# Gate blocks of one branch moved beside the mixers' small work, and moments before centring in the norms

## The chip, the cores and the metric

One core of a Trainium2 chip runs the whole kernel. The metric is the device time of one execution in microseconds (us). Three runs of the kernel before gave a median of 1899.39 us.

## The reference

Two layers of a hybrid decoder trunk work on 280 columns: 16 meta tokens, 256 prompt positions and 8 samples that each carry their own recurrent states. The stream has 1024 channels.

```python
proj = x @ w_in                       # 128 blocks of 128 columns, and dt
m_z, m_xbc, m_dt, h_q, h_f, h_i, h_g, r_q, r_k, r_v, r_g, gates = split(proj)
y_m = mamba_branch(m_z, m_xbc, m_dt, ...)      # conv, chunked recurrence, norm
y_h = hgrn_branch(h_q, h_f, h_i, h_g, ...)     # 8 heads, chunks of 32
y_r = retention_branch(r_q, r_k, r_v, r_g, ...)  # 4 heads, 256 x 512 states
g_m, g_h, g_r = split(sigmoid(gates))
mixed = g_m*(y_m @ w_br_m) + g_h*(y_h @ w_br_h) + g_r*(y_r @ w_br_r)
x = layer_norm(ALPHA*x + mixed @ w_out)
x = layer_norm(ALPHA*x + (silu(x @ w_g) * (x @ w_u)) @ w_ffn_out)
```

An input layer norm stands ahead of layer 0. All states go back to memory.

## The kernel before, in words

Channels lie on the 128 partitions and the 280 columns along the free axis; the second layer drops the 16 meta columns where it can, so that a product there has 264 columns. A weight block is 1024 x 128 values, 512 KB. `wblock` (line 204) loads it on SP's queue, ScalarE copies it to a rounded part `wh`, and VectorE subtracts to get the rest, `wl`. A block of products is 24 matmuls (wh by x, wl by x, wh by the rest of x), all from `large` (line 160). PSUM holds three such blocks (`pp`). The two layers run the same code.

**Stages of a layer.** First the convolution inputs (16 blocks, with 6 blocks of the first HGRN heads between them). Then four *pairs* p = 0 to 3 (line 1404): two HGRN heads and one Mamba-2 group are mixed, written as generators `hgrn` and `mamba`, while the projections of the next pair are computed: 6 HGRN blocks, 2 blocks of z and 2 of the HGRN gate; for p = 3 the first retention head's 8 blocks. Then retention: heads 1 to 3 are projected (8 blocks each), head by head is mixed (`ret_mix`), and `ret_samples` streams 8 states of 512 KB per head in and out of memory. In the slot of h = 3 stand the 8 blocks of the Mamba-2 branch's product (line 1445), whose results ScalarE copies out of PSUM. After them come 8 blocks of that branch's gates (`sigmoid_pair`), four multiplications on GpSimd that join the two (line 1451), the gates and product of the HGRN branch, the retention branch, the output projection, the norm, and the feed-forward layer.

**What sets the order.** `tick()` (line 260) is called in the middle and at the end of each block; each generator on the plan advances by its rate, steps over halves. `finish()` runs what is left without blocks between. The small matmuls of a step are pinned behind the large matmul issued last (`put`, line 162). The order within an engine is fixed when the program is built; an engine does not pass an instruction that waits.

**Smooth gates.** z and the HGRN gate are computed with exponentials and a logarithm (`smooth_pair`, line 819): two copies out of PSUM, then Abs, Exp, Ln on ScalarE, one two-input operation on VectorE, and Exp; z is also multiplied once more. The two blocks of z are the last but two of a pair, and the two of the HGRN gate are the last.

**Norms.** `inv_std` (line 445) squares the mean on ScalarE, takes the mean from the first two channel blocks, forms the variance, and takes the mean from the next two while ScalarE computes Ln and Exp. `scaled` (line 357) then scales block by block and splits into two parts; `opening` (line 228) starts the next stage's first three weight blocks on the channel blocks as they come. At the very end `norm` scales in place and stores.

Of the kernel before, what the change touches and what calls it, by code (L numbers as in the profile page):

```python
# [18 lines left out]
OPEN = 3  # L19
# [13 lines left out]
KB = 8  # L33
# [4 lines left out]
T = TP + NS  # L38
# [17 lines left out]
def _in_order():  # L56

    run = lambda off, n: [off + P * i for i in range(n)]
    o = []
    for p in range(4):  # L60
        heads = [c for off in (OFF_HF, OFF_HQ, OFF_HI) for c in run(off + 256 * p, 2)]
        if p == 0:
            for j, n in enumerate(MIX):
                o += run(OFF_XBC + 256 * j, 2) + heads[:n]
                del heads[:n]
        o += heads + run(OFF_Z + 256 * p, 2) + run(OFF_HG + 256 * p, 2)
    for h in range(4):
        o += run(OFF_RQ + 256 * h, 2) + run(OFF_RK + 256 * h, 2) + run(OFF_RV + 512 * h, 4)
    return o + run(OFF_GM, 8) + run(OFF_GH, 8) + run(OFF_GR, 8) + run(OFF_RG, 16)


IN_ORDER = _in_order()
# [16 lines left out]
def body(ctx: ExitStack, tc: tile.TileContext, a: dict):  # L89
# [48 lines left out]
    def copy(out, in_):  # L138
        return S.activation(out, in_, AF.Copy)  # L139
# [61 lines left out]
    fence, hold = [], []  # L201


    def wblock(src, nk):

        src_ = wraw.tile([P, RC, P], F32, tag="raw", name="raw")
        load(out=src_[:, :nk, :], in_=src)
        hi = whp.tile([P, RC, P], F32R, tag="wh", name="wh")
        lo = wlp.tile([P, RC, P], F32R, tag="wl", name="wl")
        with tc.high_priority(offset=boost):  # L210
            copy(hi[:, :nk, :], src_[:, :nk, :])
            ins = sub(lo[:, :nk, :], src_[:, :nk, :], f32(hi[:, :nk, :]))
        if fence:
            nosync(raw(ins), fence.pop())
        return hi, lo
# [7 lines left out]
            if k == nk // 2 - 1:  # L223
                tick()

    opened, norm_end = [], []

    def opening(srcs, c0):

        ps = [pp.tile([P, 512], F32, tag="pp", name="pp")[:, c0:T] for _ in srcs]  # L230
        ws = [wblock(src, KB) for src in srcs]
        for j in range(4):
            for p, w in zip(ps, ws):
                for k in (2 * j, 2 * j + 1):
                    for part in w:
                        large(p, part[:, k, :], blk(xhl[0], k)[:, c0:T], k == 0 and part is w[0], False)
        for j in range(3):
            for p, w in zip(ps, ws):
# [5 lines left out]
        opened.extend(ps)  # L244
        fence[:] = norm_end

    boost = BOOST[0]
# [109 lines left out]
    def scaled(x, rs, gk, bk, vec, less):  # L357

        nonlocal xhl
        new = tuple([pair("px", dt=F32R) for _ in range(4)] for _ in range(2))  # L360
        c = slice(lead, T)
        sca = chained()

        def full(b, e):
            xi = x[b // 2][:, b % 2, c]
            (vec if e is V else sca)(affine(xi, xi, gk, bk, b, e))

        def upper(b, e):
            xi = x[b // 2][:, b % 2, c]
            ins = (vec if e is V else sca)(affine(new[0][b // 2][:, b % 2, c], xi, gk, bk, b, e))  # L370
            if e is S:
                run["ops"].append(ins)

        def lower(j):
            return vec(sub(new[1][j][:, :, c], x[j][:, :, c], f32(new[0][j][:, :, c])))

        def times(j):
            vec(mul(x[j][:, :, c], x[j][:, :, c], b2(rs)))

        with tc.high_priority(offset=AHEAD):  # L380
            vec(mul(x[0][:, 0, c], x[0][:, 0, c], rs))
            upper(0, V)
            vec(mul(x[0][:, 1, c], x[0][:, 1, c], rs))
            upper(1, S)
            times(1)
            upper(2, S)
            upper(3, S)
            hold[:] = [run["ops"][-1]]
            full(0, V)
            less(2)  # L390
            times(2)
            full(1, S)
# [27 lines left out]
    def ln_input(x):  # L420

        first = flat("pm", P)
        G.memset(first, 1.0 / P)
        m1, mu, m2 = (mxt()[:, :T] for _ in range(3))
        mm(m1, first, x[0][:, 0, :], True, True)
        for j in range(4):
            sub(x[j], x[j], b2(m1))
            sq = pair("pm")
            S.activation(sq, x[j], AF.Square)
            if j % 2:  # L430
                total = pair("pm")
                add(total, x[j - 1], x[j])
                for i in range(2):
                    ins = mm(mu, onesd, total[:, i, :], j == 1 and i == 0, j == 3 and i == 1)
            if j < 3:
                add(sq[:, 0, :], sq[:, 0, :], sq[:, 1, :])
                mm(m2, onesd, sq[:, 0, :], j == 0, False)
            else:
                for i in range(2):
                    ins = mm(m2, onesd, sq[:, i, :], False, i == 1)  # L440
        keep_warm(14, ins)
        rs = tt_()
        scaled(x, rs, "lnin_g", "lnin_b", *inv_std(rs, mu, m2, x))

    def inv_std(rs, mu, m2, x):

        c = slice(T - rs.shape[1], T)
        vec = chained()

        def less(j):  # L450
            vec(sub(x[j][:, :, c], x[j][:, :, c], b2(mu)))

        with tc.high_priority(offset=AHEAD):
            S.activation(rs, mu, AF.Square)
            less(0)
            vec(sub(rs, m2, rs))
            vec(V.tensor_scalar(rs, rs, 0.0, None, ALU.max))
            rstd_of(rs, rs, 1.0, 0)
            less(1)
        return vec, less  # L460

    class Residual:
# [37 lines left out]
        def norm(self, gk, bk, out=None):  # L500
# [4 lines left out]
                return scaled(self.x, rs, gk, bk, vec, less)  # L505
            for j in range(4):
                x = self.x[j]
                if j > 1:
                    less(j)
                vec(mul(x[:, :, c], x[:, :, c], b2(rs)))  # L510
                for i in range(2):
                    ins = affine(x[:, i, c], x[:, i, c], gk, bk, 2 * j + i, S if i else V)
                    if i == 0:
                        vec(ins)
                store(out=out[j], in_=x[:, :, c])

    ln_input(x0)
# [292 lines left out]
    def sigmoid_pair(l, tag, silu=False):  # L810
# [5 lines left out]
                mul(t[:, i, lead:T], t[:, i, lead:T], ps)  # L816
        return t

    def smooth_pair(l, tag, silu):

        c = slice(lead, T)
        x, t = pair("pb"), pair(tag)
        for i in range(2):
            copy(x[:, i, c], in_block(l, lead))
# [555 lines left out]
    for l in range(L):  # L1380
# [20 lines left out]
        hp = hgrn_gate(l, 0, tiles)  # L1401
        z, hg = smooth_pair(l, "py", True), smooth_pair(l, "py", False)
        td = []
        for p in range(4):
# [12 lines left out]
        res = [[] for _ in range(4)]  # L1417

# [14 lines left out]

        rps = [rp]
        begin(retention(), 4 * NR, 64)
        for h in range(4):
            if h < 3:
                rps.append(ret_proj(l, h + 1, tab))
                if h == 0:
                    if l == 0:  # L1440
                        bounds()
                    begin(samples(), 4 * NSR, 122)
            else:
# [6 lines left out]
        for j in range(4):  # L1450
# [203 lines left out]
```

## Time and profile before

| | before |
|---|---|
| runs | 1896.95, 1899.39, 1900.35 us |
| the profiled execution | 1897.69 us |
| its span | 1895.6 us |
| TensorE busy (PE) | 1827.3 us |
| VectorE busy (DVE) | 1353.2 us |
| ScalarE busy (ACT) | 1090.3 us |
| GpSimd busy (POOL) | 374.6 us |
| mean granted TensorE clock | 0.989 of full speed |

The span runs from the first to the last instruction of the profiled execution; the other 2.1 us lie around it. The profiled execution is 1.7 us under the median of the runs. The granted clock has two levels in these rows: 1.00 is 2.4 GHz and 0.50 is 1.2 GHz. The order of the stages in time: the input norm to 20 us, convolution inputs to 104, pairs of layer 0 to 345, retention and merging to 725, output projection and feed-forward to 961, and the same again for layer 1.

### The profile page before, as it was taken

What the parts mean: (1) busy time and instruction counts of PE and PEld (TensorE: products, weight loads), DVE (VectorE), ACT (ScalarE), POOL (GpSimd) and SP (SyncE); (2) the same over time, 40 slices, a digit from 0 to 9 for tenths busy, and PEclk for the clock granted to TensorE, in tenths of its full rate; (3) what the DMA queues carried; (4) which work ended last, traced back from release to release, by engine and by line L of the source; (5) the groups of instructions that cost most, each with busy time, mean ns of one, the idle gap of its engine ahead of it and who ended that gap; (6) DMA issues with size and microseconds to landing.
All of it is one profiled execution on the core that took longest, in us unless ns stands there. A gap on an engine that the chain in (4) does not pass through costs nothing.

```text
span 1895.6 us, 38951 instructions
## 1 busy us (share of the span) xinstructions
PE 1827.3 (96%) x15744; PEld 1702.4 (90%) x15744; DVE 1353.2 (71%) x2183; ACT 1090.3 (58%) x1861; POOL 374.6 (20%) x415
## 2 busy tenths in 40 slices
PE   8989999999999999999999889999999999999997
PEld 7987788899888999999999778888988999999997
DVE  7898879766755766655478979996767567666654
ACT  6686677545555544544366857775455556454443
POOL 2032424211011023000220333342110100221001
PEclk9999999999999999999999989999999999999998
DMA  6545655556788744555545356555667886545563
GB/s 208 184 141 199 214 203 175 199 203 224 244 282 285 278 167 147 176 170 173 170 139 184 112 198 226 186 192 204 204 227 263 296 306 229 181 149 189 180 175 103
DMA packets 114995, 378.42 MB, mean 200 GB/s; under 512 B 13056, under 2 KB 18560, under 8 KB 114816
## 3 DMA queue, kind: packets, MB, share of 16 engines
q1 hardware_dynamic: 114816, 375.94, 59.1%
q8 instruction: 124, 2.03, 0.4%
q14 instruction: 55, 0.45, 0.1%
HBM read 317.61 MB, written 58.28 MB: 198 GB/s over the span
## 4 chain that ended last, share of the span: by engine, by line
PE 78%; DVE 11%; ACT 4%; DMA 3%; issue 2%; POOL 2%; DVEq 0%; ACTq 0%; POOLq 0%; SPq 0%
PE pp L160 63%; PE mx L169 9%; PE po L169 2%; PE vb L169 2%; DVE wl L142 2%; DVE pm L142 2%; DMA st<-s_ret 1%; DVE pa L142 1%; POOL hpt L142 1%; DMA ret_s<-st 1%; DVE py L154 1%; PE mx L172 1%; ACT wh L139 1%; DVE st L154 1%; DVE py L142 1%
## 5 line engine op out<-in xcount | busy, mean ns | idle before, releaser
L160 PE MATMUL pp<-px,wh 128*128 128x280 f32 (+1 forms) x5504 | 1119.0, 295 | 11.9 <-ACT pa L1090 5.7
L160 PEld LDWEIGHTS pp<-px,wh 128*128 128x128 f32 x5504 | 889.0, 190 | 29.8 <-issue 14.8
L142 DVE TENSOR_TENSOR wl<-raw,wh 128x1024 fp32r<-128x1024 f32 (+1 forms) x472 | 590.7, 1253 | 331.8 <-ACT wh L139 327.6
L160 PE MATMUL pp<-px,wl 128*128 128x280 f32 (+1 forms) x2752 | 796.7, 291 | 0.0
L139 ACT ACTIVATE wh<-raw 128x1024 fp32r<-128x1024 f32 (+1 forms) x472 | 493.8, 1048 | 349.8 <-PE pp L160 239.3
L160 PEld LDWEIGHTS pp<-px,wl 128*128 128x128 f32 x2752 | 521.9, 190 | 4.3 <-issue 0.8
L160 PE MATMUL pp<-py,wh 128*128 128x280 f32 (+1 forms) x1984 | 383.4, 289 | 0.8 <-ACT py L139 0.8
L160 PEld LDWEIGHTS pp<-py,wh 128*128 128x128 f32 x1984 | 313.7, 188 | 3.8 <-ACT py L139 1.3
L160 PE MATMUL pp<-py,wl 128*128 128x280 f32 (+1 forms) x992 | 285.2, 288 | 0.0
L160 PEld LDWEIGHTS pp<-py,wl 128*128 128x128 f32 x992 | 186.6, 188 | 0.7
L142 POOL TENSOR_TENSOR pa<-pa 128x280 f32<-128x280 f32 (+3 forms) x56 | 75.2, 1353 | 362.3 <-DVE pa L142 257.1
L169 PE MATMUL mx<-pm 128*32 128x16 f32 (+8 forms) x1728 | 116.6, 231 | 8.2 <-POOL pm L142 6.9
L769 ACT ACTIVATE st<-st 128x1024 f32<-128x1024 f32 x64 | 67.8, 1059 | 94.9 <-DMA st<-s_ret 62.7
L169 PEld LDWEIGHTS mx<-pm 128*32 128x32 f32 (+2 forms) x1728 | 87.5, 131 | 29.6 <-POOL pm L142 7.5
L154 DVE SCALAR_TENSOR_TENSOR st<-vb,qks,st 128x512 f32<-128x512 f32 x128 | 91.2, 745 | 23.7 <-PE vb L169 23.2
L142 DVE TENSOR_TENSOR pm<-pm 128x64 f32<-128x64 f32 (+7 forms) x179 | 85.9, 502 | 14.5 <-ACT pm L736 8.4
L142 DVE TENSOR_TENSOR pa<-pa,pp 128x280 f32<-128x280 f32 (+1 forms) x152 | 65.9, 433 | 37.0 <-PE pp L160 25.3
L142 POOL TENSOR_TENSOR pa<-px 128x560 f32<-128x560 f32 (+1 forms) x16 | 25.4, 1586 | 305.0 <-DVE py L142 304.8
L132 ACT ACTIVATE pm<-pm 128x544 f32<-128x544 f32 (+4 forms) x112 | 58.0, 540 | 13.2 <-DVE pm L154 13.1
L132 ACT ACTIVATE pa<-pp 128x280 f32<-128x280 f32 (+1 forms) x124 | 47.3, 385 | 28.8 <-PE pp L160 28.7
L139 ACT ACTIVATE pa<-pp 128x280 f32<-128x280 f32 (+1 forms) x80 | 31.4, 392 | 39.7 <-PE pp L160 39.6
L154 DVE SCALAR_TENSOR_TENSOR st<-vh,qks,st 128x128 f32<-128x128 f32 x128 | 39.7, 370 | 19.5 <-POOL st L142 11.7
(252 smaller groups left out, 1871.9 us busy)
## 6 DMA issues: line engine op xcount, KB each, us to landing
raw<-w_in SPq DMA_DIRECT2D x256, 512.0 KB
raw<-w_ffn_in SPq DMA_DIRECT2D x88, 512.0 KB
st<-s_ret SPq DMA_DIRECT2D x64, 512.0 KB
ret_s<-st SPq DMA_DIRECT2D x64, 512.0 KB
vh<-rows SPq DMA_DIRECT2D x64, 256.0 KB
raw<-w_br_r SPq DMA_DIRECT2D x32, 512.0 KB
raw<-w_ffn_out SPq DMA_DIRECT2D x32, 512.0 KB
st<-s_ssm SPq DMA_DIRECT2D x16, 512.0 KB
```

The costliest lines, as they stand in the source:

```text
L132: ins = S.activation(out, in_, func, **kw)
L139: return S.activation(out, in_, AF.Copy)
L142: return e.tensor_tensor(out, x, y, op)
L154: return V.scalar_tensor_tensor(out, x, s, y, op0, op1)
L160: place[0] = raw(TE.matmul(out, lhsT, rhs, start=start, stop=stop, skip_group_check=True))
L169: return put(TE.matmul(out, lhsT, rhs, start=start, stop=stop, skip_group_check=True))
L172: return put(TE.transpose(out, x, ident))
L769: S.activation(st, st, AF.Copy, scale=gam)
```

## The change

The input weights are stored in a new order, and so are the blocks. After the blocks of z and the HGRN gate of pairs 1 to 3 stand two blocks of the Mamba-2 branch's gates, and the last two stand after the first retention head. They are only copied out of PSUM (`plain_pair`); a new generator turns them into gates by the smooth way while retention head 1 is projected. The product of the Mamba-2 branch moves from the slot of h = 3 to h = 1, ahead of the projection of head 2, and is multiplied into the gates straight from PSUM. The rates follow: the pairs' generators run over 23 halves for 19, the retention's samples over 106 for 122. In the norms the variance is formed before any mean is taken off, and the second subtraction moves behind the first scaling. The input norm centres all four blocks in another order and issues the first three weight blocks itself, two behind the last square and one behind the last exponential. The last norm puts most of its scaling on ScalarE.

```diff
 (_in_order, pairs)
         o += heads + run(OFF_Z + 256 * p, 2) + run(OFF_HG + 256 * p, 2)
+        if p:
+            o += run(OFF_GM + 256 * (p - 1), 2)
     for h in range(4):
+        if h == 1:
+            o += run(OFF_GM + 768, 2)
...
 (wblock)
-            copy(hi[:, :nk, :], src_[:, :nk, :])
+            ins = copy(hi[:, :nk, :], src_[:, :nk, :])
+            if behind_ is not None:
+                nosync(raw(ins), raw(behind_))
 (opening)
-        ws = [wblock(src, KB) for src in srcs]
+        ws = ahead or [wblock(src, KB) for src in srcs]
 (scaled)
             upper(1, S)
+            less(1)
             times(1)
 (ln_input)
+        centre(0)
+        centre(1)
+        mean(0)
+        centre(2)
+        centre(3)
+        squares(0)
+        mean(1)
+        squares(1)
+        squares(2)
+        for i in range(2):
+            ins = mm(m2, onesd, sq[3][:, i, :], False, i == 1)
+        last_sq = squared[-1]
+        ahead.extend(wblock(a["w_in"][0, b], KB, last_sq) for b in range(OPEN - 1))
         keep_warm(14, ins)
         rs = tt_()
-        scaled(x, rs, "lnin_g", "lnin_b", *inv_std(rs, mu, m2, x))
+        how = inv_std(rs, mu, m2, x)
+        fence[:] = norm_end
+        ahead.append(wblock(a["w_in"][0, OPEN - 1], KB, run["ops"][-1]))
+        scaled(x, rs, "lnin_g", "lnin_b", *how)
 (inv_std)
             S.activation(rs, mu, AF.Square)
-            less(0)
             vec(sub(rs, m2, rs))
             vec(V.tensor_scalar(rs, rs, 0.0, None, ALU.max))
             rstd_of(rs, rs, 1.0, 0)
-            less(1)
+            norm_end[:] = [less(0)]
 (norm, the last)
-                if j > 1:
-                    less(j)
                 vec(mul(x[:, :, c], x[:, :, c], b2(rs)))
+                if j < 3:
+                    less(j + 1)
                 for i in range(2):
-                    ins = affine(x[:, i, c], x[:, i, c], gk, bk, 2 * j + i, S if i else V)
+                    ins = affine(x[:, i, c], x[:, i, c], gk, bk, 2 * j + i, V if i == 0 and j == 3 else S)
 (the layer)
-            begin(hgrn(l, p, hp, hg, oh), NH, 19)
-            begin(mamba(l, p, td, dd, xm, bc, z, ym), NM + 2 * (p == 0), 19)
+            begin(hgrn(l, p, hp, hg, oh), NH, 23)
+            begin(mamba(l, p, td, dd, xm, bc, z, ym), NM + 2 * (p == 0), 23)
             if p < 3:
                 hp = hgrn_proj(l, p + 1)
                 z, hg = smooth_pair(l, "py", True), smooth_pair(l, "py", False)
+                gm.append(plain_pair(l, pair("py")))
                 finish()
             else:
...
                 rp = ret_proj(l, 0, tab)
+                gm.append(plain_pair(l, pair("py")))
...
+        def gates_m():
+            for j in range(4):
+                for _ in range(2):
+                    yield 1
+                x, t = gm[j], pair("py")
+                smooth(x, t)
+                gm[j] = t
         for h in range(4):
+            if h == 0:
+                gms = begin(gates_m(), 8, 14)
+            if h == 1:
+                while len(ym) < 4 or gms in plan:
+                    tick()
+                block = branch(l, a["w_br_m"], ym)
+                for b in range(8):
+                    g = gm[b // 2][:, b % 2, lead:T]
+                    mul(g, g, block(b))
             if h < 3:
                 rps.append(ret_proj(l, h + 1, tab))
...
-                    begin(samples(), 4 * NSR, 122)
-            else:
-                mixed = pairs("pa", 4)
-                block = branch(l, a["w_br_m"], ym)
-                for b in range(8):
-                    copy(blk(mixed, b)[:, lead:T], block(b))
+                    begin(samples(), 4 * NSR, 106)
         boost = BOOST[2]
-        gm = gates(l)
-        for j in range(4):
-            mul(mixed[j][:, :, lead:T], mixed[j][:, :, lead:T], gm[j][:, :, lead:T], G)
+        mixed = gm
```

## Rows read from the trace of the kernel before

**Rows 1.** The page: busy time, share of the span and instructions of each engine.
```profile
PE 1827.3 (96%) x15744; PEld 1702.4 (90%) x15744; DVE 1353.2 (71%) x2183; ACT 1090.3 (58%) x1861; POOL 374.6 (20%) x415
```

**Rows 2.** Windows: stretch, its length, busy time by engine, granted clock, DMA share, GB/s.
```profile
core 0: us, PE busy (x) PEld busy (x) DVE busy (x) ACT busy (x) POOL busy (x), PEclk, DMA share, GB/s
100.00:345.00 245.00, 228.18 (x2521) 196.99 (x2520) 213.31 (x436) 169.57 (x379) 88.64 (x88) 0.98 0.57 191
1040.00:1305.00 265.00, 245.39 (x2643) 211.69 (x2642) 235.94 (x470) 186.17 (x409) 95.21 (x99) 0.96 0.57 192
655.00:725.00 70.00, 70.00 (x545) 69.76 (x544) 45.23 (x52) 34.71 (x43) 12.95 (x8) 1.00 0.51 172
```

**Rows 3.** Waits of PE over the span: who waited for whom, us in total, times, longest.
```profile
PE mx L169 <- DVE pm L142: 10.8, 7, 4.3
PE po L172 <- DVE pq L142: 7.3, 4, 2.7
PE mx L169 <- POOL pm L142: 6.9, 4, 4.2
PE pp L160 <- ACT pa L1090: 5.7, 2, 4.5
...
PE mx L172 <- ACT pm L139: 2.8, 2, 2.4
```

**Rows 4.** Windows of PE alone: the stretches of the mixers at half clock.
```profile
179.19:182.61 3.42, 3.42 (x16) 0.50 0.25 63
231.60:237.22 5.62, 5.62 (x18) 0.50 0.31 117
...
1094.90:1100.79 5.89, 5.66 (x31) 0.50 0.17 67
...
sum 28.59, PE 28.36; mean PE 4.05
```

**Rows 5.** Timeline at the end of pair 1: start, us, engine, line, operation, idle before.
```profile
223.30 1.90 POOL L142 TENSOR_TENSOR st<-st,dab 128x1024 f32<-128x1024 f32 x1
223.47 2.33 DVE L142 TENSOR_TENSOR py<-py 128x560 f32<-128x560 f32 x1
...
231.60 2.21 PE L169 MATMUL mx<-pm,ones 128*128 128x280 f32 x4 [4.27 <-DVE pm L142]
```

**Rows 6.** Timeline at the start of pair 1.
```profile
178.01 0.74 DVE L154 SCALAR_TENSOR_TENSOR py<-pb,py 128x560 f32<-128x560 f32 x1 [0.41 <-ACT py L132]
...
179.13 0.59 PE L172 MATMUL po<-ident,pa 128*32 128x128 f32 x2 [2.19 <-DVE pq L142]
```

**Rows 7.** Groups of instructions over the span: busy us, mean ns, idle before.
```profile
L142 DVE TENSOR_TENSOR wl<-raw,wh 128x1024 fp32r<-128x1024 f32 (+1 forms) x472 | 590.7, 1253 | 331.8 <-ACT wh L139 327.6
...
L142 DVE TENSOR_TENSOR pa<-pa,pp 128x280 f32<-128x280 f32 (+1 forms) x152 | 65.9, 433 | 37.0 <-PE pp L160 25.3 <-ACT pa L132 10.9
...
L132 ACT ACTIVATE py<-py,eps 128x560 f32<-128x560 f32 (+1 forms) x16 | 11.9, 745 | 0.1
```

**Rows 8.** The chain that ended last, in the feed-forward layer: start, us, what.
```profile
765.09 195.13 PE pp L160 x1512
```

**Rows 9.** Windows at the start and in the second layer's sample states; columns as in Rows 2.
```profile
5.00:10.00 5.00, 2.51 (x6) 1.78 (x6) 4.77 (x10) 2.29 (x4) 0.00 (x0) 1.00 1.01 341
...
1440.00:1593.00 153.00, 152.80 (x1266) 138.76 (x1266) 102.10 (x132) 88.34 (x126) 13.56 (x10) 1.00 0.85 293
```

**Rows 10.** Timeline of the input norm.
```profile
16.38 2.35 DVE L142 TENSOR_TENSOR wl<-raw,wh 128x1024 fp32r<-128x1024 f32 x2
...
19.71 0.37 PE L160 MATMUL pp<-px,wh 128*128 128x280 f32 x1 [2.30 <-DVE px L343]
```

**Rows 11.** Timeline of the norm between the layers.
```profile
962.17 0.74 DVE L142 TENSOR_TENSOR pa<-pa,mx 128x560 f32<-128x560 f32 x1 [0.99 <-ACT tt L454]
...
971.11 0.39 PE L160 MATMUL pp<-px,wh 128*128 128x280 f32 x1 [0.25 <-ACT px L342]
```

**Rows 12.** Timeline of the last norm, VectorE.
```profile
1883.78 0.70 DVE L142 TENSOR_TENSOR pa<-pa,mx 128x528 f32<-128x528 f32 x1 [0.93 <-ACT tt L454]
...
1891.62 0.42 DVE L343 TENSOR_SCALAR pa<-pa,par 128x264 f32<-128x264 f32 x1
```

More of the change, by code (lines that the diff above doesn't have):

```diff
@@ L66, in _in_order @@
         o += heads + run(OFF_Z + 256 * p, 2) + run(OFF_HG + 256 * p, 2)
+        if p:
+            o += run(OFF_GM + 256 * (p - 1), 2)
     for h in range(4):
+        if h == 1:
+            o += run(OFF_GM + 768, 2)
         o += run(OFF_RQ + 256 * h, 2) + run(OFF_RK + 256 * h, 2) + run(OFF_RV + 512 * h, 4)
-    return o + run(OFF_GM, 8) + run(OFF_GH, 8) + run(OFF_GR, 8) + run(OFF_RG, 16)
+    return o + run(OFF_GH, 8) + run(OFF_GR, 8) + run(OFF_RG, 16)
 IN_ORDER = _in_order()
@@ L201, in body, with wblock @@
     fence, hold = [], []
-    def wblock(src, nk):
+    def wblock(src, nk, behind_=None):
         src_ = wraw.tile([P, RC, P], F32, tag="raw", name="raw")
@@ L224, in project @@
                 tick()
-    opened, norm_end = [], []
+    opened, norm_end, ahead = [], [], []
     def opening(srcs, c0):
         ps = [pp.tile([P, 512], F32, tag="pp", name="pp")[:, c0:T] for _ in srcs]
-        ws = [wblock(src, KB) for src in srcs]
+        ws = ahead or [wblock(src, KB) for src in srcs]
         for j in range(4):
@@ L244, in opening @@
         opened.extend(ps)
+        ahead.clear()
         fence[:] = norm_end
@@ L425, in ln_input, with centre, mean, squares @@
         mm(m1, first, x[0][:, 0, :], True, True)
-        for j in range(4):
[L427 to L437, printed above, removed]
-            else:
-                for i in range(2):
-                    ins = mm(m2, onesd, sq[:, i, :], False, i == 1)
+        vec = chained()
+        sq, total = pairs("pm", 4), pairs("pm", 2)
+        squared = []
+        def centre(j):
+            vec(sub(x[j], x[j], b2(m1)))
+            squared.append(S.activation(sq[j], x[j], AF.Square))
+        def mean(j):
+            vec(add(total[j], x[2 * j], x[2 * j + 1]))
+            for i in range(2):
+                mm(mu, onesd, total[j][:, i, :], i + j == 0, i + j == 2)
+        def squares(j):
+            vec(add(sq[j][:, 0, :], sq[j][:, 0, :], sq[j][:, 1, :]))
+            mm(m2, onesd, sq[j][:, 0, :], j == 0, False)
+        centre(0)
[7 more added lines that the diff above has]
+        squares(2)
+        for i in range(2):
+            ins = mm(m2, onesd, sq[3][:, i, :], False, i == 1)
+        last_sq = squared[-1]
+        ahead.extend(wblock(a["w_in"][0, b], KB, last_sq) for b in range(OPEN - 1))
         keep_warm(14, ins)
         rs = tt_()
-        scaled(x, rs, "lnin_g", "lnin_b", *inv_std(rs, mu, m2, x))
+        how = inv_std(rs, mu, m2, x)
+        fence[:] = norm_end
+        ahead.append(wblock(a["w_in"][0, OPEN - 1], KB, run["ops"][-1]))
+        scaled(x, rs, "lnin_g", "lnin_b", *how)
     def inv_std(rs, mu, m2, x):
@@ L450, in less @@
         def less(j):
-            vec(sub(x[j][:, :, c], x[j][:, :, c], b2(mu)))
+            return vec(sub(x[j][:, :, c], x[j][:, :, c], b2(mu)))
         with tc.high_priority(offset=AHEAD):
             S.activation(rs, mu, AF.Square)
-            less(0)
             vec(sub(rs, m2, rs))
@@ L507, in norm @@
                 x = self.x[j]
-                if j > 1:
-                    less(j)
                 vec(mul(x[:, :, c], x[:, :, c], b2(rs)))
+                if j < 3:
+                    less(j + 1)
                 for i in range(2):
-                    ins = affine(x[:, i, c], x[:, i, c], gk, bk, 2 * j + i, S if i else V)
-                    if i == 0:
-                        vec(ins)
+                    ins = affine(x[:, i, c], x[:, i, c], gk, bk, 2 * j + i, V if i == 0 and j == 3 else S)
                 store(out=out[j], in_=x[:, :, c])
@@ L817, in sigmoid_pair, with plain_pair, smooth @@
         return t
+    def plain_pair(l, x):
+        for i in range(2):
+            copy(x[:, i, lead:T], in_block(l, lead))
+        return x
     def smooth_pair(l, tag, silu):
+        return smooth(plain_pair(l, pair("pb")), pair(tag), silu)
+    def smooth(x, t, silu=False):
         c = slice(lead, T)
-        x, t = pair("pb"), pair(tag)
-        for i in range(2):
-            copy(x[:, i, c], in_block(l, lead))
         S.activation(t[:, :, c], x[:, :, c], AF.Abs)
@@ L1403, in body @@
         td = []
+        gm = []
         for p in range(4):
-            begin(hgrn(l, p, hp, hg, oh), NH, 19)
-            begin(mamba(l, p, td, dd, xm, bc, z, ym), NM + 2 * (p == 0), 19)
+            begin(hgrn(l, p, hp, hg, oh), NH, 23)
+            begin(mamba(l, p, td, dd, xm, bc, z, ym), NM + 2 * (p == 0), 23)
             if p < 3:
@@ L1441, in body @@
                         bounds()
-                    begin(samples(), 4 * NSR, 122)
-            else:
-                mixed = pairs("pa", 4)
-                block = branch(l, a["w_br_m"], ym)
-                for b in range(8):
-                    copy(blk(mixed, b)[:, lead:T], block(b))
+                    begin(samples(), 4 * NSR, 106)
         boost = BOOST[2]
-        gm = gates(l)
-        for j in range(4):
-            mul(mixed[j][:, :, lead:T], mixed[j][:, :, lead:T], gm[j][:, :, lead:T], G)
+        mixed = gm
         yh = [split(o) for o in oh]
```

## The prediction

> **What bounds the kernel now.** I read the page's busy times first, then windows by stage, then PE's waits, then the timeline around the longest of them. TensorE is busy for 1827.3 of 1895.6 us [rows 1], and the change neither adds nor drops a matmul of a block: 24 matmuls follow each other at 195.13 / 1512 = 0.129 us, 3.1 us a block, wherever nothing small lies between [rows 8]. So a gain can only come from idle or slow TensorE. The windows show where that is: in the pairs of layer 0 PE is busy for 228.2 of 245 us and in those of layer 1 for 245.4 of 265, 16.8 + 19.6 = 36.4 us idle, while a stretch in the late gates has none [rows 2]. The mean clock of both pair stages is below 1.00 as well. Seven stretches, each right after a long wait, run at 0.50, that is 1.2 GHz, 28.6 us in all [rows 4]; at full clock the same work takes half of that, so they cost up to 14.3 us. The two together, 50.7 us, are what the pair stages have to give.
>
> The waits by partner [rows 3], with the 2.5 us of the input norm taken off the first row, and half of each slow stretch [rows 4] put to the wait that it follows, make four sorts:
> - *Before the pairs*: waits for ACT at L1090, 5.7 us, with one slow stretch of 3.4 us: 5.7 + 1.7 = 7.4 us.
> - *At the start of a pair*: a transpose into the shared PSUM tile waits for DVE's `pq`, 7.3 us in 4 waits, and another for ACT's `pm`, 2.8 us; four slow stretches of 3.4 us follow: 10.1 + 6.8 = 16.9 us.
> - *At the end of a pair*: the sums of squares of the norms wait for DVE, 10.8 - 2.5 = 8.3 us, with one slow stretch of 5.6 us: 8.3 + 2.8 = 11.1 us.
> - *In the middle*: matmuls wait for GpSimd's products, 6.9 us, with one of 5.9 us: 6.9 + 2.9 = 9.8 us.
>
> **The change part by part.** *Gate blocks in the pairs.* Each pair gets two blocks more, 6.2 us of TensorE, taken from the late gates, where PE never idles: the work itself nets to zero. Each block brings its load on SP's queue (512 KB at a DMA share of 0.57 [rows 2], 4.2 MB a layer), a ScalarE copy and a subtraction of 1.25 us on DVE [rows 7]. DVE is busy for 213 of 245 us there [rows 2]; a pair gets 2.5 us more of it beside 6.2 us of PE. The generators' steps now come every 23/17 = 1.35 halves for 1.12.
>
> By counting ticks from the code, a start-of-pair wait changes like this. Mamba's second step, whose DVE results are awaited, stays on tick 3; HGRN's third step, whose transpose waits, goes from tick 4 to tick 5: another half block, 1.56 us, lies between. The second reason is in the timeline: DVE reaches `pq` late since the smooth operation of the gate just projected stands in front of it and itself waits 0.41 us for ACT; PE then waits 2.19 us [rows 6]. With the two plain blocks last in a pair, that chain (Abs, Exp, Ln of 0.75 us [rows 7], the DVE operation of 0.74 us, Exp) is over two blocks earlier. Bounds: no gain, or all 16.9 us. I take three quarters, 12.7, as spacing alone covers 1.56 of each wait and a wait that falls away takes its slow stretch with it.
>
> End of a pair: the last steps keep their spacing in ticks (square to sum is two ticks before and after), but the smooth chains no longer fall among them. DVE's backlog there has another part, though: an operation that takes 2.33 us beside a GpSimd product on the states, against 0.74 us for a like one elsewhere [rows 5, 11]. That stays. Bounds 0 and 11.1; I take half, 5.5. Middle: the steps from GpSimd's products to their readers lie 4 ticks apart, as before; bounds 0 and 9.8, I take 2. Before the pairs nothing changes: 0. Against this stand new waits that a new order brings: nothing in the trace shows them; the bounds are nothing and the longest wait but one, 4.2 us [rows 3], in each layer. I take 3 for both. Net: -12.7 - 5.5 - 2 + 3 = -17.2 us.
>
> *Smoothing, product and joining.* The gates take four two-block chains a layer: four ScalarE operations of at most 0.75 us [rows 7] and one of 0.74 us on DVE [rows 6] each, spread over 16 halves of retention head 1. They replace eight sigmoids. The product's eight multiplications read PSUM at 0.43 us each on DVE [rows 7] for eight ScalarE copies, and GpSimd loses four. DVE and ACT have time in those stages; cost 0. Without this cover it would be 8 x 0.43 = 3.5 us a layer. The loop that waits for the Mamba results and the gates turns zero times: 20 + 16 = 36 ticks have passed and the slower generator needs 23. Of the 22 `py` slots I count at most 21 in use.
>
> *Retention order and samples.* Head 2 is projected 8 blocks later, so one slot of 16 halves has no retention steps, and head 3 is mixed beside the HGRN gates; these are blocks all the same, 0. The samples run 36 steps in 106 halves for 122: 2.94 halves a step. Per step that is 1.05 MB of states and 1.47 blocks of 0.52 MB, 1.82 MB. At 3.39 halves and 293 GB/s a step now takes (1.05 + 0.89) MB / 293 = 6.6 us, 1.3 more than its 3.39 x 1.56 us of blocks: that is the small matmuls. So in samples alone a step will take 2.94 x 1.56 + 1.3 = 5.9 us, at 309 GB/s against 293 at a share of 0.85 now, in a stretch with 0.2 us of PE idle; the start of the kernel moved 341 at a share of 1.01 [rows 9]. There is room, but less. Bounds 0 and 12 us (below); I take +1.5.
>
> *Input norm.* PE starts its first block at 19.71; two subtractions, 2.35 us, stand in DVE's way just before [rows 10]. By an estimate from those rows the first block could start some 3.1 us earlier: 1.6 us of the two subtractions lie behind the exponential, 0.66 us come from the variance's new place (as below), and some 0.8 from sums that end earlier and a ScalarE that is free for Ln. But the third weight's subtraction (1.2 us) and one centring (0.7 us) now fall into the chain that feeds the later channel blocks. 3.1 - 1.9 = 1.2; I take -1.3, as a short cast (0.1 us of it) leaves that chain (bounds -3.1 and +0.5).
>
> *Norms within.* The variance no longer waits for a centring of 0.74 us [rows 11], 0.66 us as its successor starts: the first matmul comes 0.66 earlier. But one centring of 0.73 us comes back between the first and the second scaling. PE's later wait, at 971.11 for the seventh channel block [rows 11], is fed by that chain: 0.07 us later. Three norms: +0.2 (bounds -2 and +2).
>
> *Last norm.* Its chain loses the same 0.66 us and three scalings on DVE (0.42 us long, about 0.35 each in the chain), and gains a centring of 0.70 [rows 12]: -0.66 - 1.05 + 0.70 = -1.0 (bounds -1.7 and 0).
>
> **Sum.** -17.2 + 1.5 - 1.3 + 0.2 - 1.0 = -17.8 us. The profiled execution took 1897.7, its span and 2.1 us around it: 1879.9. The median of the runs is 1.7 above the profiled execution: 1881.6, rounded to 1882.
>
> **The rivals.** *Blocked by GpSimd.* The 2.33 us at the end of pair 1 begin 0.17 us after GpSimd's product of 1.90 us and end 0.6 us after it [rows 5]. If such blocking, and not the smooth chains, makes DVE late, it stays, since the change moves none of the products on the states. Then only the spacing pays, at the start of pairs, on the four waits for `pq`: 1.56 off each of three and all of the shortest, 0.67, which makes 5.3 us, and two slow stretches, 3.4; less 3 for new waits, and -0.6 for all other parts: 1897.7 - 6.3 + 1.7 = 1893. For it: these rows. Against: where PE waits at 179 us DVE was held by ACT, not by GpSimd [rows 6]. The Trainium skill has a rule for this (SBUF — State Buffer, Who interferes with whom): VectorE with two SBUF inputs and a GpSimd instruction that reads SBUF share one port pair, and the second to issue is blocked until the first is done. By that rule the end-of-pair waits stay at 11.1 us and the forecast loses 5.5; the trace agrees with it for this one instruction.
>
> *All of it.* Start, end and middle waits vanish, 37.8 us, nothing new comes: 1897.7 - 37.8 - 0.6 + 1.7 = 1861. For it: DVE is not full. Against: the middle steps keep their spacing.
>
> *Nothing.* New waits in another order eat the gain: 1899. The sum's +3 would have to be 20.
>
> *Slower: the samples' stream.* The 58 halves of a layer with samples alone take 116 us by the step above and carry 35.9 MB. If the queue does not deliver 309 GB/s, weights come late on SP's queue, behind loads that wait for a free state buffer, and PE waits. The gain of 17.8 us, 8.9 a layer, is gone if the stream takes 125 us, at 287 GB/s; at 280 it takes 128.2, +12.2 a layer: 1881.6 + 24.4 = 1906. For it: the share is 0.85 already. Against: 293 GB/s are moved now without idle on PE, 341 elsewhere.
>
> **How the numbers follow.** Chances: forecast 0.55, blocked 0.19, all 0.08, nothing 0.09, slower 0.09. The range 1866 to 1897 leaves out about half of "all" and of "nothing", and "slower". A measurement of this kernel tells 0.2%, 3.8 us, from no change, so faster means below 1895.6: 0.55 + 0.08 + 0.17 of "blocked" = 0.80; same 0.11; slower 0.09.
>
> **What would show it.** The windows of the pairs grow by 25 us a layer less the gain, with PE idle down from 36 to 20 us or less and two or three slow stretches for seven; no wait for `pq` over 1.2 us. If the waits at the end of pairs are still 4 us, "blocked" is right. In the sample stage the share should read about 0.9, with PE idle under 5 us a layer; waits of `pp` for `wh` or `wl` there would mean the stream. The last norm should be 1 us shorter. The prediction is wrong if the pair stages keep over 30 us of idle.

## The result, and the profile after

The change takes 1874.43 us (median of four runs, 1874.11 to 1875.70) against 1899.37 us before (four runs, 1896.95 to 1900.35): a ratio of 0.9877, interval 0.9859 to 0.9894. Faster was the forecast, at 1882; the gain is 25 us where 17.4 were forecast. The profiled execution is the one of 1874.11 us, with a span of 1872.1, against 1897.69 and 1895.6 before.

The page of after, busy time by engine:

```profile
PE 1824.7 (97%) x15744; PEld 1699.4 (91%) x15744; DVE 1357.1 (72%) x2204; ACT 1109.3 (59%) x1880; POOL 376.6 (20%) x407
```

TensorE does the same work [rows 1]; the 23.5 us of span were idle or slow time. Windows of after: the pairs of layer 0, those of layer 1, and the stretch of layer 1 with sample states and blocks alone. Columns as in [rows 2].

```profile
100.00:360.00 260.00, 253.53 (x2754) 223.03 (x2753) 225.45 (x449) 185.48 (x400) 95.15 (x88) 1.00 0.62 205
1027.00:1300.00 273.00, 260.25 (x2781) 227.51 (x2780) 238.88 (x463) 193.79 (x416) 105.62 (x94) 0.97 0.58 198
1472.00:1558.00 86.00, 85.91 (x715) 76.64 (x714) 57.49 (x79) 50.55 (x67) 5.30 (x4) 1.00 0.87 305
```

Idle PE in the pairs is 6.5 us in layer 0 and 12.8 in layer 1; it was 16.8 and 19.6. In this execution layer 0 has no time at half clock any more; layer 1 has 17.0 us of it in the pairs and 3.4 in retention, where it had 19.6 in the pairs [rows 4]. From the first block of a layer to the first of the next (for layer 1, to the end of its last block) the time fell from 946.0 to 929.4 us in layer 0, but only from 916.2 to 912.4 in layer 1. One profile does not fix this split, as the experiment on the product's place shows. PE's waits over the span of after, columns as in [rows 3]:

```profile
PE pp L164 <- ACT pa L1119: 5.7, 2, 4.5
PE po L176 <- DVE pq L146: 5.6, 3, 2.0
PE mx L173 <- POOL pm L873: 3.6, 1, 3.6
PE vb L173 <- DVE st L158: 3.2, 2, 2.3
PE mx L176 <- DVE pm L158: 3.1, 4, 0.8
PE mx L173 <- DVE pm L146: 2.8, 2, 2.3
...
PE mx L173 <- POOL pm L146: 2.4, 1, 2.4
PE mx L173 <- POOL pa L646: 1.7, 1, 1.7
```

Of the waits for DVE's `pm`, 10.8 us in seven before, 2.8 are left, 2.25 of them in the input norm: the waits at the ends of pairs are gone from this execution. The three for `pq` are all in layer 1. The stretches of after at half clock (1.2 GHz), PE alone:

```profile
1037.40:1047.60 10.20, 9.51 (x69) 0.50 0.32 104
1177.30:1180.70 3.40, 3.40 (x18) 0.50 0.85 260
1272.90:1276.30 3.40, 3.40 (x19) 0.50 0.65 217
1402.60:1406.00 3.40, 3.40 (x18) 0.50 0.73 267
```

Why `pq` still comes late in layer 1 is in the timeline of after ahead of one such wait (start, us, engine, line, operation):

```profile
1109.92 2.10 POOL L146 TENSOR_TENSOR st<-st,dab 128x1024 f32<-128x1024 f32 x1
1110.18 2.92 DVE L146 TENSOR_TENSOR wl<-raw,wh 128x1024 fp32r<-128x1024 f32 x1
...
1113.49 0.39 PE L176 MATMUL po<-ident,pa 128*32 128x128 f32 x2 [2.03 <-DVE pq L146]
```

The subtraction for `wl` takes 2.92 us where its mean was 1.25 [rows 7]: it begins 0.26 us after GpSimd's product on the states and ends about 1.1 us after it. DVE then has `pq` behind it. Ahead of the two other waits a 128 x 272 operation that takes 0.43 us elsewhere takes 2.14 and 2.15 us beside such a product, some 8 us earlier, and DVE works on almost without a pause from there to `pq`.

### The profile page after: what moved, and what is told of

Its sections match the earlier page's. It is cut to its first block, busy times and chain, and to the rows that moved or that the text cites. A ratio compares the mean times of both kernels' runs of the same rounds, so it can differ in the third digit from the quotient of the medians.

```text
span 1872.1 us, 38981 instructions
## 1 busy us (share of the span) xinstructions
PE 1824.7 (97%) x15744; PEld 1699.4 (91%) x15744; DVE 1357.1 (72%) x2204; ACT 1109.3 (59%) x1880; POOL 376.6 (20%) x407
## 3 DMA queue, kind: packets, MB, share of 16 engines
q8 instruction: 124, 2.03, 0.4%
## 4 chain that ended last, share of the span: by engine, by line
PE 71%; DVE 6%; ACT 3%; DMA 1%; issue 1%; POOL 0%; ACTq 0%; DVEq 0%; SPq 0%
PE pp L164 59%; PE mx L173 7%; PE po L173 2%; PE vb L173 2%; DVE pa L146 1%; DVE wl L146 1%; DVE pm L146 1%; DMA st<-s_ret 1%; PE mx L176 1%; DVE py L158 0%; ACT px L349 0%; DMA pm<-c_dec 0%; ACT wh L143 0%; DVE pm L1166 0%; DVE py L146 0%
## 5 line engine op out<-in xcount | busy, mean ns | idle before, releaser
L164 PEld LDWEIGHTS pp<-px,wh 128*128 128x128 f32 x5504 | 888.6, 189 | 32.0 <-issue 12.5
L146 DVE TENSOR_TENSOR wl<-raw,wh 128x1024 fp32r<-128x1024 f32 (+1 forms) x472 | 597.6, 1268 | 326.0 <-ACT wh L143 325.0
L146 POOL TENSOR_TENSOR pa<-pa 128x280 f32<-128x280 f32 (+3 forms) x40 | 47.6, 1206 | 208.4 <-DVE pa L146 197.7
L136 ACT ACTIVATE pa<-pp 128x280 f32<-128x280 f32 (+1 forms) x108 | 41.5, 385 | 31.7 <-PE pp L164 31.6
L173 PE MATMUL po<-st,qd 128*32 128x256 f32 x640 | 53.4, 394 | 0.1
L146 POOL TENSOR_TENSOR st<-st,hfc 128x1024 f32<-128x1024 f32 x16 | 32.8, 2047 | 96.3 <-DMA st<-s_hgrn 39.7
```

The lines of the kernel that those rows point to most:

```text
L136: ins = S.activation(out, in_, func, **kw)
L146: return e.tensor_tensor(out, x, y, op)
L164: place[0] = raw(TE.matmul(out, lhsT, rhs, start=start, stop=stop, skip_group_check=True))
L173: return put(TE.matmul(out, lhsT, rhs, start=start, stop=stop, skip_group_check=True))
```

## The experiments

All times are medians beside runs of the kernel before on the same chip (1897 to 1898 us). By theory *spacing*, the wider distance of the generators' steps carries the gain; by theory *GpSimd*, VectorE is late because its operations are stretched beside GpSimd's products on the states.

**The norms alone**, on the kernel before.

```diff
 (kernel before)
+ln_input, inv_std, norm, scaled, wblock, opening: as in the change
```

> The kernel before with the edits to the norms alone (input norm, order of variance and centring, last norm). Theory A (the pairs of mixers carry the gain): the two ends of the kernel gain what they gained in the change, 1.9 us at the input and 1.2 at the last norm, and the inner norms nothing: 1896 (+-1). Theory B (the norms carry much of it, by starting each stage earlier): under 1890.

1897.34 us, ratio 0.9991 (0.9976 to 1.0005): not to be told from nothing. Theory B is out.

**The change without the norms.**

```diff
 (the change)
-ln_input, inv_std, norm, scaled, wblock, opening: as in the kernel before
```

> The change without its edits to the norms. Theory A: all of the stages' gain stays, 1874.4 + 3 = 1877.5 (+-1.5). Theory B: over 1884.

1878.32 us, ratio 0.9899 (0.9880 to 0.9919). What is left, the gate blocks, the product's place and the rates, carries the gain.

**The change at the old rate of the pairs.**

```diff
-            begin(hgrn(l, p, hp, hg, oh), NH, 23)
-            begin(mamba(l, p, td, dd, xm, bc, z, ym), NM + 2 * (p == 0), 23)
+            begin(hgrn(l, p, hp, hg, oh), NH, 19)
+            begin(mamba(l, p, td, dd, xm, bc, z, ym), NM + 2 * (p == 0), 19)
```

> The change with the pairs' generators back at 19 halves for 23: steps as dense as before, and the last four halves of a pair, its plain gate blocks, have no steps. Theory 'spacing' (the waits went since more of a block lies between two steps): most of the waits come back, 1874 + 10 to 15 = 1884 to 1889. Theory 'order' (they went since the smooth chains of z and gate no longer stand at a pair's end and start): the steps end four halves early and the waits at starts stay short: 1872 to 1878.

1894.44 us, ratio 0.9978 (0.9958 to 0.9997): most of the gain is gone, more than theory *spacing* gave, though the gate blocks stand in the pairs. In the profiles the loss lies there: the 46 blocks from the start of pair 0 on took 16.8 us more than in after in layer 0 and 7.5 in layer 1, and the span grew by 23.9. PE's waits in this kernel:

```profile
PE mx L173 <- POOL pm L146: 8.5, 5, 3.4
PE po L176 <- DVE pq L146: 7.2, 4, 2.5
PE vb L173 <- DVE st L158: 6.9, 4, 3.3
PE mx L173 <- DVE pm L146: 6.3, 5, 2.3
```

The waits for `pq` are back at 7.2 us (7.3 before [rows 3]), those for GpSimd are at 8.5. Blocks in a pair do little, some 4 us, if the steps don't spread over them.

**The gate blocks ahead of z and the HGRN gate**, so that the smooth chains come last in a pair as before.

```diff
 (the layer; in _in_order the blocks change places likewise)
...
-                z, hg = smooth_pair(l, "py", True), smooth_pair(l, "py", False)
                 gm.append(plain_pair(l, pair("py")))
+                z, hg = smooth_pair(l, "py", True), smooth_pair(l, "py", False)
```

> The change with the two gate blocks of a pair ahead of the blocks of z and the HGRN gate, so that the smooth chains are last in a pair as before; rates as in the change. Theory 'order': the waits at starts and ends of pairs come back, 1874 + 10 to 15 = 1884 to 1889. Theory 'spacing': 1873 to 1877.

1876.55 us, ratio 0.9890 (0.9867 to 0.9913): not to be told from the change. PE's waits in the pairs of layer 0 (130 to 345 us) of this kernel; after has there only the one wait for GpSimd, 2.4 us at 335.5:

```profile
PE mx L174 <- DVE pm L147: 1.8, 2, 1.2
PE mx L174 <- POOL pm L147: 1.5, 1, 1.5
PE po L177 <- DVE pq L147: 0.2, 1, 0.2
```

The waits at the ends, 1.8 us in two, are no mark of this order. The kernel with the product at h = 3, below, leaves the instructions of layer 0's pairs in the order of after, on every engine; its profile shows nearly the same two waits there, and a stretch at half clock (columns as for the stretches of after) that after has not:

```profile
PE mx L173 <- DVE pm L146: 2.0, 2, 1.2
```

```profile
337.30:340.60 3.30, 2.90 (x12) 0.50 0.95 379
```

So what the order of the smooth chains does can't be seen, and no start wait of layer 0 but 0.2 us came back with it.

**The samples at their old rate.**

```diff
-                    begin(samples(), 4 * NSR, 106)
+                    begin(samples(), 4 * NSR, 122)
```

> The change with the samples' generator at 122 halves again for 106. Theory 'the denser stream costs little': 1874 to 1876, the waits for the samples' sums (3.2 us) no shorter than now. Theory 'the denser stream eats gain': 1870 to 1872, with those waits and the DMA share in the sample stage down.

1897.24 us, ratio 0.9992 (0.9977 to 1.0008): a miss for both theories, and the whole gain lost. In retention of layer 0 (345 to 560 us) PE's waits for the mixing of a head read, in this kernel and then in after:

```profile
PE mx L176 <- DVE pm L158: 6.8, 3, 3.9
```

```profile
PE mx L176 <- DVE pm L158: 1.4, 2, 0.7
```

In layer 1 they are 7.0 against 1.7. At the longest of them DVE alternates the head's `pm` with the sample states' 0.74 us updates, and PE waits 3.9 us; three stretches at half clock, 17 us, lie in the retention stages too, for one of 3.4 in after. So the denser samples are no cost to be borne: without them the change gains nothing. Why is not shown. Counted from the code, 136 halves lie between the samples' start and the block that needs the last head's in the kernel before, and 120 in the change, so 122 fits the first and not the second; in layer 0 the last matmul on these states begins at 656.8 us here and at 624.7 in after. Of the 24.0 us by which the span is longer than after's, 5.5 lie in the pairs, though their instructions stand in after's order; what the rest is made of stays open. The samples at 106 in the kernel before were not run, so what that rate gives by itself is not known.

**The product back in the slot of h = 3**, still multiplied straight into the gates.

```diff
-            if h == 1:
+            if h == 3:
                 while len(ym) < 4 or gms in plan:
                     tick()
...
```

> The change with the Mamba-2 product back in the slot of h = 3 (still multiplied into the gates), so only the gate blocks are moved. Theory 'the pairs carry the gain': 1874 to 1877. Theory 'the product's place beside the second head's mixing gives part of it': 1879 or more.

1872.94 us, ratio 0.9880 (0.9861 to 0.9899): the product's place carries nothing that can be told. The profiled span is 1871.9 us, next to after's 1872.1, but here layer 0 took 935.9 us and layer 1 905.9: 10.1 and 10.3 less than before, not 16.6 and 3.8, with the pairs of both layers in after's order.

**The state products on VectorE.**

```diff
-            mul(s4, s4, dab[:, 4 * c:4 * c + 4, heads].unsqueeze(3).to_broadcast([P, 4, 4, 64]), G)
+            mul(s4, s4, dab[:, 4 * c:4 * c + 4, heads].unsqueeze(3).to_broadcast([P, 4, 4, 64]))
...
-            mul(st, st, fb, G)
+            mul(st, st, fb)
```

> The change with the products on the Mamba and HGRN states (four a pair, 128 x 1024) on VectorE for GpSimd. Theory 'blocked' (what is left of the waits at the pairs' starts in the second layer comes from DVE operations that GpSimd's products hold up): DVE pays some 1.2 us a product but loses the 1.3 to 1.7 us of each blocked operation, the waits for pq go under 1 us each, 1868 to 1873. Theory 'load' (DVE simply has too much there): four times 1.2 us more in a pair, waits grow, 1877 to 1884.

1866.92 us, ratio 0.9850 (0.9828 to 0.9871), though DVE gets 32 operations of 1.2 us more (16 on the Mamba-2 samples' states and 16 on the HGRN samples'; the expectations of the two last runs call the latter retention's). That is just below what theory *blocked* gave; its interval still touches the change's. The scan in the pairs of layer 0 (count, min/median/max ns, first and last start), in after and then here:

```profile
L1166 DVE TENSOR_TENSOR_SCAN pm<-ones,pa x8: 694/708/2440, 109.7 to 293.5; 128x272 f32<-128x272 f32 x8
```

```profile
L1166 DVE TENSOR_TENSOR_SCAN pm<-ones,pa x8: 698/709/721, 107.3 to 290.3; 128x272 f32<-128x272 f32 x8
```

No scan is stretched any more, and in the pairs of layer 1 (1045 to 1300 us) PE's only waits are for GpSimd; `pq` is not among them:

```profile
PE mx L173 <- POOL pm L146: 4.0, 3, 2.7
```

**Pair 0's smooth chains taken off the queue and onto the plan**, aimed at the 4.5 us wait ahead of the pairs of layer 1.

```diff
-        z, hg = smooth_pair(l, "py", True), smooth_pair(l, "py", False)
+        zx, hx = plain_pair(l, pair("py")), plain_pair(l, pair("py"))
+        z, hg = pair("py"), pair("py")
+
+        def late(zx, hx, z, hg):
+            for x, t, silu in ((zx, z, True), (hx, hg, False)):
+                for _ in range(2):
+                    yield 1
+                smooth(x, t, silu)
+
+        begin(late(zx, hx, z, hg), 4, 12)
```

> The change with the smoothing of z and gate of pair 0 put on the plan, nine and fifteen halves into the pair, for running ahead of it. Theory 'ACT's queue' (the waits ahead of the pairs, 1.1 and 4.5 us with the slow stretch of 10.2 us behind the second, come from this chain standing in ACT's queue ahead of the copies out of PSUM): the 4.5 us and the slow stretch go in good part, 1865 to 1870. Rival (the extra HGRN gate work of the second layer holds ACT and DVE there): 1873 to 1876.

1882.52 us, ratio 0.9924 (0.9906 to 0.9942): slower than the change by some 8 us, and outside what either theory gave. PE's longest waits from 1026 to 1100 us:

```profile
PE mx L173 <- POOL pm L146: 4.2, 2, 4.0
PE po L176 <- ACT pq L143: 2.1, 1, 2.1
PE pp L164 <- DVE wl L146: 1.9, 1, 1.9
```

The wait was cut up and moved into the pair, with the chains.

**The second layer's lower-bound terms left out**, in the change and in the kernel before; these are eight operations per pair of layer 1's HGRN gate.

```diff
 (hgrn_gate)
-        if l > 0:
+        if l > L:
```

> The change, with the second layer's HGRN gate computed as the first layer's: its lower-bound terms (per pair some VectorE and ScalarE operations of layer 1) are left out. To be read against the kernel before with the same left out (e8). Theory W (work): the change takes only 3.8 us out of layer 1 and 16.5 out of layer 0 because layer 1's longer gate fills the time that the wider spacing gives; without it, layer 1 from its first block to the last matmul is about 12 us shorter than in e8 and the two runs together lie about 32 us apart. Theory G (GpSimd): the waits that layer 1 keeps come from VectorE operations lengthened beside GpSimd's state products, whatever the gate; waits of 1.5 to 2.5 us for pq stay at the starts of pairs 1 to 3 of layer 1, this run is within 3 us of 1875 - 2, and e7 and e8 lie about 25 us apart.

> The kernel before with the same lower-bound terms left out; the partner of e7. Theory W: VectorE's lead is no longer short in layer 1 only where spacing was added, so before gains little here: 1892 to 1897. Theory G: the same small gain, 1893 to 1897, and e7 gains as little. The difference between e7 and e8 decides, not this run alone; if this run falls to 1885 or lower, the gate was what cost layer 1 its waits in both kernels.

1872.78 us for the change, 1894.86 for the kernel before: ratios 0.9869 (0.9854 to 0.9885) and 0.9981 (0.9961 to 1.0001), 22.1 us apart; with the terms, the two lie 25 apart. Theory W wanted 32, and by the times it is out. Its other sign, a layer 1 about 12 us shorter than its partner's, nearly came: 902.4 against 912.1 in the profiled executions, 9.7 us, where 3.8 lie between them with the terms. PE's longest waits in the pairs of layer 1, first of the change so cut (1050 to 1300 us), then of the kernel before so cut (1070 to 1320 us):

```profile
PE mx L173 <- DVE pm L146: 4.0, 3, 2.0
PE mx L173 <- POOL pa L646: 1.9, 1, 1.9
```

```profile
PE mx L169 <- DVE pm L142: 7.2, 4, 2.6
PE mx L169 <- POOL pm L142: 2.5, 2, 1.3
```

Theory G wanted the waits for `pq` to stay, and misses as well: they are gone from both kernels, and PE waits for `pm` at the ends of pairs instead. The totals hardly move, by 1.5 and 2.8 us. Layer 0, from which nothing was left out, took 7 us longer in both of these executions than in those of after and before (936.5 for 929.4, 953.3 for 946.0), so the layers' times decide nothing. Less work on DVE and ACT shifted the place where PE waits; that it removed the lateness is not shown.

**The state products on VectorE in the kernel before**: the same two lines.

> The kernel before with the state products of the Mamba-2 samples and the retention samples on VectorE instead of GpSimd, nothing else. Theory G alone (the waits at the starts of pairs are VectorE operations lengthened beside GpSimd, and spacing only shifts them apart): it gains about what the change gains, 1870 to 1880. Theory S (spacing carries the change's 20 us; GpSimd is a second, smaller cause): it gains what the same edit gained on top of the change, 6 to 10 us: 1887 to 1891. If VectorE's queue was the bound in the short spacing, it gains nothing or loses: 1897 to 1903.

1881.02 us, ratio 0.9914 (0.9902 to 0.9926): twice what theory S gave it and just short of theory G. PE's waits in the pairs of layer 0 (130 to 345 us), at the old spacing and the old order of blocks:

```profile
PE mx L169 <- POOL pm L142: 0.6, 1, 0.6
PE mx L172 <- DVE pm L154: 0.4, 1, 0.4
```

Start and end waits are both gone from there, and from the first block to the output projection layer 0 took 21.6 us less. Layer 1 took 6.7 us more. Its matmuls on the sample states (1020 to 1320 us; count, busy us, mean ns), before and then here:

```profile
L169 PE MATMUL po<-st,qd 128*32 128x256 f32 x64 | 5.6, 422 | 0.0
L169 PE MATMUL vb<-st,qd 128*32 128x128 f32 x128 | 5.2, 279 | 0.0
```

```profile
L169 PE MATMUL vb<-st,qd 128*32 128x128 f32 x128 | 11.6, 282 | 0.0
L169 PE MATMUL po<-st,qd 128*32 128x256 f32 x64 | 10.0, 391 | 0.0
```

The order of instructions that came with this edit puts large matmuls between them, one or two at a time, and the two groups occupy PE for 10.8 us more; over all instructions PE is busy for 234.5 us in the 38 blocks of those pairs, before 223.2.

**The state products on VectorE and the product at h = 3**: the edits of two experiments above together.

> The change with the state products on VectorE and with the Mamba-2 branch's product left in the slot of h = 3 (still multiplied straight from PSUM). Products on VectorE gave 7.5 us and the product's place gave 1.5 +- 4 apart from each other. Theory 'independent': 1862 to 1867. Rival: at h = 3 the eight multiplications out of PSUM fall on a VectorE that now carries the retention states as well, and the pp buffers come free later: 1868 to 1873.

1866.40 us, ratio 0.9836 (0.9819 to 0.9853): the fastest of all, its interval below the change's, as theory *independent* had it. Against the state products alone it can't be told apart. Its partner with the products on GpSimd is the change with the product at h = 3, at 0.9880: there the state products on VectorE gain some 8 us, clear of both intervals.

## Why the prediction was right, step by step

The direction and most of the size were right. By the prediction's own sorts (waits, and half of the slow stretch behind each):

| | before | forecast | after |
|---|---|---|---|
| before the pairs | 7.4 | 7.4 | 5.7 + 5.1 = 10.8 |
| start of a pair | 16.9 | 4.2 | 5.6 + 1.7 = 7.3 |
| end of a pair | 11.1 | 5.6 | 0.5 |
| in the middle | 9.8 | 7.8 | 4.1 + 1.7 = 5.8 |

The four give -20.8 us where -20.2 was forecast; the new waits taken at +3 were mostly not there (PE's waits in retention are 6.3 us for 6.8, with one slow stretch more). That the four sums meet so closely is in part luck: the last column is one execution, and the profile with the product at h = 3 adds 2.0 us of end waits and a slow stretch in layer 0. Of the signs named ahead, PE idle in the pairs came down to 19.3 us, where 20 or less was asked, and the slow stretches there to three for seven, 17.0 us of 28.6; but waits for `pq` of 1.7 to 2.0 us stay in layer 1, where none over 1.2 was to be. Two halves were mis-sized in opposite ways:

- *Start of a pair.* Of its two reasons, spacing holds: at the old rate `pq` waits are back. The second, that smooth chains no longer come last, does not carry: with the chains last again the time is the same within its interval, and the starts of layer 0 stay clean. The 4.2 left was too little: 7.3 us are there, all in layer 1.
- *End of a pair.* The step said that DVE's stretch beside GpSimd "stays", and left half of the 11.1 us. The stretching stayed: after has a scan of 2.44 us in layer 0, whose median is 0.71. The waits did not, or only 2.0 us of them in the other profile: with 1.35 halves between steps the stretched operation mostly ends in time. (Of the 8.3 us before, 6.4 are waits of sums of squares, at 231.60 and 292.51 us; another, 1.24 at 124.41, is not at the end of a pair, and its 0.5 in after neither.)
- *Before the pairs.* The wait is the same 4.5 us; the half-clock stretch behind it was 10.2 us instead of 3.4. The sorts left out a wait that seems to go with its length: before, PE stood 2.5 us for ACT's `pq` 12.5 us later, in pair 0 of layer 1, and in after it does not. In the change without the norms the stretch is 3.4 us again, in after's order, and that wait is 3.0.
- *Blocked by GpSimd* was put down as a rival that would keep the gain to 6 us. As an outcome it was wrong, as a cause it was in part right. Taking the products off GpSimd in the kernel before removes the start waits of layer 0 too, for which the prediction had named ACT and the smooth chain. Its reading of the wait at 179 us, that DVE was held by ACT and not by GpSimd, stopped one step short. In the kernel before, ACT had itself stood for DVE 5 us earlier:

```profile
171.41 2.09 POOL L142 TENSOR_TENSOR st<-st,dab 128x1024 f32<-128x1024 f32 x1 [3.05 <-DMA st<-s_ssm]
171.66 2.99 DVE L154 SCALAR_TENSOR_TENSOR py<-py,par,tm 128x280 f32<-128x280 f32 x3
...
174.26 0.67 ACT L139 ACTIVATE py<-py 128x560 fp32r<-128x560 f32 x1 [2.96 <-DVE py L154]
```

  One such DVE operation takes 0.51 us at 175.62; these three, begun 0.25 us behind a GpSimd product, take 2.99, and the smooth chain stands behind them in ACT's queue. The two edits repair in part the same thing:

| ratio to before | products on GpSimd | on VectorE |
|---|---|---|
| order and spacing of before | 1 | 0.9914 |
| of the change | 0.9877 | 0.9850 |

Added up, 1.23% and 0.86% would be 2.09%; together they give 1.50%. So some 11 us of what the change gains (with intervals of 0.12 to 0.22% on each ratio, about 5 to 17) is time that the other edit gives back too: by the traces above, time that VectorE lost beside GpSimd. The rest it gains even without that. The figure is rough, since both edits also reorder instructions, and in the kernel before that made layer 1's state matmuls dearer. The Trainium skill's rule (SBUF — State Buffer, Who interferes with whom: VectorE with two SBUF inputs and a GpSimd instruction that reads SBUF exclude each other) is borne out by the scan's 2.44 us, begun 0.35 us behind a product and ended 0.6 us after it, and 0.72 at most without the products on GpSimd. It prices the operation and not the kernel: what a stretch costs depends on the distance to its reader.

- *Samples.* Over the last two heads' 16 steps in layer 1 a step takes 5.71 us, before 6.40; 5.9 and 6.6 were forecast. They move 305 GB/s at a share of 0.87 with PE idle for 0.1 us [rows 9]: no stream rival. That the old rate loses everything was not foreseen.
- *Input norm.* Forecast -1.3, measured about 0. The opening of after:

```profile
17.85 0.37 PE L164 MATMUL pp<-px,wh 128*128 128x280 f32 x1
...
21.20 0.39 PE L164 MATMUL pp<-px,wh 128*128 128x280 f32 x1 [0.65 <-ACT px L349]
...
22.97 0.40 PE L164 MATMUL pp<-px,wh 128*128 128x280 f32 x1
```

and the start of the second block before:

```profile
23.12 0.40 PE L160 MATMUL pp<-px,wh 128*128 128x280 f32 x1
```

  The first matmul comes 1.86 us earlier [rows 10], the second block 0.15. PE starts sooner and meets the later channel blocks, which are no sooner there.
- *Norms within.* The same in small: in the three norms the first block starts 0.4 to 0.55 us earlier, and from the second block on PE is 0.14 to 0.28 us later, +0.6 for the three; +0.2 was forecast.
- *Last norm.* From the end of the last block to the end of the span 13.67 us became 12.46: -1.2 for the forecast -1.0. With the two above that makes -0.7, and the norms alone measured -0.6.

Open: how the gain divides between the layers. After's profile says 16.6 and 3.8 us, the one with the product at h = 3 says 10.1 and 10.3. With the second layer's terms left out, layer 0 of the change runs after's instructions in after's order on all engines, and yet took 7 us longer. So a difference of 7 us in one layer between two single profiles does not show the effect of an edit. What stays in layer 1 in each of these is the wait of 4.5 us ahead of the pairs, which was not removed at a gain; its waits for `pq` go with the state products, and with the left-out terms.

## What to carry to other kernels

Where PE waits for a short chain on another engine, look at the distance in large matmuls between the step and its reader before its operations: blocks moved beside the chain help only as far as the chain's steps are spread over them. When a wait disappears, ask whether its cause did: here the stretched VectorE operations stayed, and taking GpSimd's competing products away gave more on top. Before a wait in a profile is put down to an edit, look at the same stage in another kernel that runs it in the same order. Judge an earlier start by the second block, not the first.

## What the runs showed of the hardware that was not expected

A tiny operation is stretched as well. In after's timeline a 128 x 4 TENSOR_SCALAR, which takes 0.16 or 0.17 us in six of its eight places (and 0.19 at most in all eight with the state products on VectorE), takes 1.70 us when it begins 0.23 us behind a GpSimd product, though only one tensor goes into it:

```profile
170.21 1.90 POOL L146 TENSOR_TENSOR st<-st,dab 128x1024 f32<-128x1024 f32 x1 [1.00 <-DMA st<-s_ssm]
170.44 1.70 DVE L1230 TENSOR_SCALAR hnc<-pm 128x4 f32<-128x4 f32 x1
```

And the half-clock stretch behind a wait is not set by the length of the wait: 4.51 us at the same place was followed by 3.4 us of it before and by 10.2 after, and by 3.4 in the change without the norms, in after's order; waits of 1.89 and 1.74 us in layer 1 of after were each followed by 3.4, those of 2.03 and 1.69 by none.
